# The second layer's output projection, the order of its weights and rows, and the empty rows of the expert scatter

## The chip, the core and the metric

The kernel runs on one core of a Trainium2 chip. The metric is the device time of one execution in microseconds; the time before is the median of three runs. The figures of the profile come from one more execution, recorded by the hardware profiler. TensorE (PE) multiplies, ScalarE (ACT) casts and activates, VectorE (DVE) and GpSimd (POOL) do element work, SyncE (SP) issues most of the loads; ACT and POOL issue DMAs too, POOL the indexed ones.

## The reference, cut to what matters

Two layers work on 256 latent and 256 context rows of 1024 numbers. The first layer keeps all 512 rows, the second only the 256 latent ones, which are two tiles of 128 rows (tiles 2 and 3 of the kernel). Each layer has a mixer and routed experts:

```python
gate_a, gate_b, gate_c = jnp.split(jax.nn.sigmoid(gates), N_BRANCH, axis=-1)
branch_a = (y_a @ w_glu_val) * jax.nn.sigmoid(y_a @ w_glu_gate)
m = gate_a * branch_a + gate_b * (y_b @ w_proj_gm) + gate_c * (y_c @ w_proj_da)
mix = m @ w_out                                     # w_out is 1024 x 1024
...
h_lat = layer_norm(DN_ALPHA * h_lat + g1 * mix_lat, ln1_g[l], ln1_b[l])
f_lat = modulate(layer_norm(h_lat), sh2, sc2)
# 8 of 64 experts for each row of f, each with 256 hidden units
y = sum_e weight_e * (silu(f @ w_gate[e]) * (f @ w_up[e])) @ w_down[e]   + shared expert
h_lat = layer_norm(DN_ALPHA * h_lat + g2 * y_lat, ln2_g[l], ln2_b[l])
```

## The kernel before

Dense products are made in three matmuls (`mm3`, L135 to L137): each operand is split into a rounded high part, cast by ACT, and the rest, subtracted by DVE or POOL (hi times hi, lo times hi, hi times lo). So a weight that is loaded must be cast and subtracted before PE can use it. `wload` takes a buffer of a pool with two buffers named `raw`, 8 KB per partition each, and the load into a buffer waits until the casts and subtractions of its last content are over; `wsplit` makes `whi` and `wlo`, two buffers each, out of it. Both are written by the tile framework: an engine runs its instructions in the order in which the scheduler wrote them, and waits by semaphore.

The mixer's end has three passes over eight output blocks o0 to o7 of 128 columns (`gates`): X=1, then X=0 (gate a, with w_glu_gate and w_glu_val), then X=2 (gate c, with w_proj_da, 12 matmuls of `ych`, `ycl` in each block). Each pass streams 4 MB of w_in, in four 1 MB loads of two blocks each, through the two `raw` buffers; tanh of the gate is written to `gt`. Pass X=2 leaves the sum of the three branches in `mh`, `ml`, the operand of w_out.

In the second layer w_out comes in halves of 512 columns. Half 1 is loaded by `out_weights` in four 512 KB pieces through two other buffers, `mraw`, which the modulation's weights had used; it is cast and subtracted into `wo` beside the first blocks of X=0. Half 0 is loaded after X=2's last w_in piece (two 1 MB pieces), through `raw`, and split two k-rows at a time in `whi`, `wlo`. The matmuls of both halves into the PSUM tiles `opp` run for each k as `mh` comes, a few in each block of X=2, the rest behind its last block. Then `residual` makes r = 2^0.5 h + g1 * opp in two 512-column pieces for each tile, with pieces `op_h` of the rows of h loaded for it, and `out_proj` makes both layer norms, the router's scores (sigmoid, L1041), and f, which is stored. The constants ln_g, ln_b, sh, sc are loaded from ACT's queue behind its last cast.

Routing then writes tables: `t_gather` (which row of f each of a tile's 128 places reads) and `t_scatter` (to which row of `acc` its result is added). An expert tile is two lanes of 64 places, one expert each; an expert's rows fill whole lanes, the rest of a lane stays empty. Empty places read nothing (their gather index is beyond the bounds) and scatter to 64 dump rows behind each lane's part of `acc`. For each tile, DVE copies the weights from the ring (`raw`, four slots of 3 MB, one expert each) into `gu` and `dn`, PE transposes xg (L1566), multiplies (`pg`, L1575), transposes `sg` into `ph` (L1584) and multiplies again (`py`, L1592); POOL adds the tile's 128 rows to `acc` with an indexed DMA (L1595), and SP reloads ring slots as they come free.

## Time and profile before

| | us |
|---|---|
| three runs | 2009.74, 2008.34, 2000.35 |
| median | 2008.34 |
| the profiled execution | 2000.67 |
| its span | 1998.8 |
| layer-1 mixer, 1250 to 1552 | 302 |
| its norms and router, 1552 to 1580 | 28 |
| routing, to 1618 | 38 |
| layer-1 experts, 1618 to 1957 | 339 |
| layer-0 experts, 633 to 1180 | 547 |

The profiled execution is beside the fastest of the three runs; 7.67 us lie between it and the median. Each stage is one stretch of the timeline. A wait row tells how long an engine stood still and whose event ended it. The clock column is the share of full speed that TensorE was granted: 1.00 is 2.4 GHz, 0.50 is 1.2 GHz.

### The profile page before, as it was taken

How to read it: one execution, taken by the hardware profiler on the slowest of the kernel's cores; microseconds unless marked ns; L12 is line 12 of the kernel's file. 1: busy time of each engine (PE TensorE's matmuls, PEld its weight loads, DVE VectorE, ACT ScalarE, POOL GpSimd, SP SyncE). 2: the span in 40 equal slices, each digit the busy share in tenths (PEclk: the TensorE clock that was granted, in tenths of full speed). 3: DMA queues.
4: the chain of work that ended last, by engine and by line, in shares of the span. 5: the costliest groups of instructions: out<-in, count | busy, mean ns of one | idle time of the engine just before them, and what ended most of it. 6: DMA issues, size and time to landing. Idle time of an engine off the chain costs nothing. (4 is left out here: it accounts for less than half of the span.)

```text
span 1998.8 us, 30455 instructions
## 1 busy us (share of the span) xinstructions
PE 1792.3 (90%) x10137; PEld 1040.6 (52%) x10137; DVE 1176.3 (59%) x2346; ACT 595.6 (30%) x1139; POOL 528.3 (26%) x407
## 2 busy tenths in 40 slices
PE   5798999999998999999998974989989689998894
PEld 2686876778765333333333323767789443333331
DVE  7687554333666666666665637823563666646563
ACT  3343343332222222222222215423453212221211
POOL 4354301222311222222222224321143012232221
PEclk8898999999999999999999976979999799999986
DMA  8113524453778677787898957346544379999974
GB/s 276 49 44 115 176 95 140 150 193 130 269 248 314 198 214 210 228 292 232 301 323 293 381 168 263 119 156 214 194 145 169 142 299 309 317 304 388 377 259 116
DMA packets 168310, 440.11 MB, mean 220 GB/s; under 512 B 26261, under 2 KB 82995, under 8 KB 151226
## 3 DMA queue, kind: packets, MB, share of 16 engines
q1 hardware_dynamic: 132044, 340.89, 46.6%
q0 software_dynamic: 20448, 62.41, 13.7%
q10 hardware_dynamic: 15630, 34.56, 4.8%
q8 instruction: 86, 1.41, 0.3%
q14 instruction: 102, 0.84, 0.1%
HBM read 658.36 MB, written 58.17 MB: 358 GB/s over the span
## 5 line engine op out<-in xcount | busy, mean ns | idle before, releaser
L1575 PE MATMUL pg<-gu,xt 128*64 128x512 f32 x2176 | 497.4, 610 | 1.5 <-ACT xt L1567 1.5
L1544 DVE COPY gu<-raw 128x1024 f32 x560 | 364.1, 694 | 207.8 <-SPq L1237 97.0
L1575 PEld LDWEIGHTS pg<-gu,xt 128*64 128x64 f32 x2176 | 153.8, 140 | 298.0 <-issue 283.7
L1595 POOL DMA_INDIRECT acc<-y,t_scatter x68 | 124.3, 1828 | 606.6 <-ACT ht L1585 430.0
L1592 PE MATMUL py<-dn,ht 128*64 128x512 f32 x1088 | 251.3, 604 | 5.4 <-ACT ht L1585 5.4
L1550 DVE COPY dn<-raw 128x2048 f32 x140 | 172.0, 1229 | 120.0 <-PE py L1592 100.5
L135 PE MATMUL mm<-uh,whi 128*128 128x512 f32 (+1 forms) x544 | 198.6, 365 | 6.8 <-ACT rx L848 4.6
L137 PE MATMUL mm<-uh,wlo 128*128 128x512 f32 (+1 forms) x544 | 194.9, 359 | 0.5 <-DVE wlo L314 0.5
L136 PE MATMUL mm<-ul,whi 128*128 128x512 f32 (+1 forms) x544 | 193.7, 356 | 0.0
L314 DVE TENSOR_TENSOR wlo<-raw,whi 128x1024 fp32r<-128x1024 f32 x77 | 97.8, 1271 | 114.1 <-ACT whi L311 113.9
L1579 ACT ACTIVATE sg<-pg 128x256 f32<-128x256 f32 x68 | 26.1, 384 | 452.1 <-PE pg L1575 452.1
L1524 POOL DMA_INDIRECT xg<-f,t_gather x74 | 101.0, 1365 | 180.8 <-DMA acc<-sh_y 56.2
L1592 PEld LDWEIGHTS py<-dn,ht 128*64 128x64 f32 x1088 | 72.8, 138 | 132.5 <-issue 118.7
L1594 ACT ACTIVATE y<-py,w 128x512 f32<-128x512 f32 x136 | 93.5, 687 | 161.2 <-PE py L1592 161.2
L311 ACT CAST whi<-raw 128x1024 fp32r<-128x1024 f32 x92 | 96.0, 1047 | 146.3 <-PE mm L136 117.7
L135 PEld LDWEIGHTS mm<-uh,whi 128*128 128x128 f32 x544 | 106.1, 195 | 31.7 <-issue 6.4
L137 PEld LDWEIGHTS mm<-uh,wlo 128*128 128x128 f32 x544 | 105.7, 194 | 18.5 <-issue 4.5
L136 PEld LDWEIGHTS mm<-ul,whi 128*128 128x128 f32 x544 | 106.0, 195 | 17.1 <-issue 4.5
L1566 PEld LDWEIGHTS px<-ct,xg 128*128 128x128 f32 x560 | 67.9, 194 | 57.4 <-issue 55.7
L1566 PE MATMUL px<-ct,xg 128*128 128x128 f32 x560 | 81.0, 288 | 0.9 <-DMA xg<-f,t_gather 0.9
L1567 ACT COPY xt<-px 128x512 f32<-128x512 f32 x140 | 75.3, 590 | 18.9 <-PE px L1566 17.9
L145 POOL TENSOR_TENSOR rs_r<-rs_ve,eps 128x1 f32<-128x1 f32 (+1 forms) x38 | 31.1, 822 | 178.5 <-DVE rs_ve L143 150.9
(473 smaller groups left out, 2738.8 us busy)
## 6 DMA issues: line engine op xcount, KB each, us to landing
raw<-in_w_exp_gate_dram SPq DMA_DIRECT2D x148, 1024.0 KB
raw<-in_w_exp_up_dram SPq DMA_DIRECT2D x148, 1024.0 KB
raw<-in_w_exp_down_dram SPq DMA_DIRECT2D x148, 1024.0 KB
raw<-in_w_in_dram SPq DMA_DIRECT2D x42, 1024.0 KB
mraw<-in_w_mod_dram SPq DMA_DIRECT2D x80, 512.0 KB
fraw<-in_w_mod_dram SPq DMA_DIRECT2D x16, 512.0 KB
cb_y<-acc SPq DMA_DIRECT2D x12, 512.0 KB
pj<-in_w_proj_da_dram SPq DMA_DIRECT2D x8, 512.0 KB
```

The source lines that it names most:

```text
L135: nc.tensor.matmul(out, lh, rh, start=start, stop=False)
L136: nc.tensor.matmul(out, lh, rl, start=False, stop=False)
L137: self.last = nc.tensor.matmul(out, ll, rh, start=False, stop=stop).ins
L311: self.nc.scalar.copy(hv, src)
L314: i = eng.tensor_tensor(lv, src, hv.bitcast(F32), op=ALU.subtract)
L1524: nc.gpsimd.indirect_dma_start(out=XG[t % AHEAD], out_offset=None, in_=fD, in_offset=bass.IndirectOffsetOnAxis(ap=tb["gather"][:, t:t + 1] ...
L1544: c = V.tensor_copy(GU[ln][b], gu[:, 2 * b:2 * b + 2])
L1550: c = V.tensor_copy(DN[ln][t % 2].rearrange("p a b -> p (a b)"), srcs[ln][:, 4096:6144])
L1566: nc.tensor.transpose(pX[hf][:, k * P:(k + 1) * P], XG[t % AHEAD][:, 4 * hf + k:D:8], ident)
L1575: nc.tensor.matmul(pG[t % 2][r, :], XT[t % 2][:, k, r], GU[ln][k // 2][:, k % 2].rearrange("p g n -> p (g n)"), start=(k == 0), stop=(k == ...
L1592: nc.tensor.matmul(pY[hf][r, :], HT[:, k, r], DN[ln][t % 2][:, k, 512 * hf:512 * hf + 512], start=(k == 0), stop=(k == 1), tile_position=( ...
L1595: nc.gpsimd.indirect_dma_start(out=acc, out_offset=bass.IndirectOffsetOnAxis(ap=tb["scatter"][:, t:t + 1], axis=0), in_=Y[t % 2], in_offse ...
```

## The change

In the second layer both halves of w_out are loaded and split ahead of pass X=2, in eight 512 KB pieces through the two `raw` buffers that also carry w_in. All matmuls of tile 2 are written ahead of those of tile 3. The rows of h are two tiles of 128 x 1024, and both residual pieces of a tile stand in `out_proj`. A one-column sigmoid `op_sg` behind the first tile's first norm brings ACT's table load there. In both layers the dump rows of `acc` are gone: an empty place gets an index beyond `acc` and the scatter skips it by its bounds. w_exp_down is loaded with the rows p*2 and p*2+1 in partition p, one 8 KB run; the transposes of `SG` take every second column to match.

```diff
--- before.py
+++ after.py
...
...
@@ -978,13 +977,16 @@
             nc.scalar.dma_start(dst[:, 512 * hf:512 * hf + 512], y)
             yield
 
-    def out_first(self, l, pool, tiles):
-
-        half = dict(r={}, sm={}, g={})
+    def out_first(self, l, pool, tiles, h_tiles):
+
+        half = dict(r={}, sm={}, g={}, h={})
         for s in sorted(set(t // 2 for t in tiles)):
             half["g"][s] = self.mod_bc(pool, l, 0, s, "g1_%d" % s)
         for t in tiles:
             half["r"][t] = pool.tile([P, D], F32, name="op_r%d" % t)
+            if l == DEPTH - 1:
+                half["h"][t] = pool.tile([P, D], F32, name="op_h%d" % t)
+                self.nc.sync.dma_start(half["h"][t], h_tiles[t])
             half["sm"][t] = pool.tile([P, 2], F32, name="op_sm%d" % t)
         return half
 
@@ -992,13 +994,16 @@
 
         V = self.nc.vector
         c = slice(512 * hf, 512 * hf + 512)
-        h = pool.tile([P, 512], F32, name="op_h", bufs=2 if self.l < DEPTH - 1 else 4)
-        self.nc.sync.dma_start(h, h_tile[:, c])
+        if t in half["h"]:
+            h = half["h"][t][:, c]
+        else:
+            h = pool.tile([P, 512], F32, name="op_h", bufs=2)
+            self.nc.sync.dma_start(h, h_tile[:, c])
         r = half["r"][t][:, c]
         V.tensor_mul(r, ps, half["g"][t // 2][:, c])
         V.scalar_tensor_tensor(r, h, ALPHA, r, op0=ALU.mult, op1=ALU.add, accum_out=half["sm"][t][:, hf:hf + 1])
 
-    def out_proj(self, l, pool, pp, mh, ml, wh, wl, ps1, half, tiles, t0, h_tiles, h1_tiles, f_tiles, fT, rt):
+    def out_proj(self, l, pool, pp, mh, ml, wh, wl, ps0, ps1, half, tiles, t0, h_tiles, h1_tiles, f_tiles, fT, rt):
 
         nc, A = self.nc, self.A
         V = nc.vector
@@ -1019,11 +1024,16 @@
                 ps = pp.tile([P, 512], F32, name="mm", tag="mm", bufs=2)
                 self.out_half(ps, mh, ml, wh, wl, c0)
                 self.paced(TAIL[0])
+            if l == DEPTH - 1:
+                self.residual(pool, half, t, 0, ps0[t], h_tiles[t])
             self.residual(pool, half, t, 1, ps, h_tiles[t])
             r = half["r"][t]
             sm = pool.tile([P, 1], F32, name="op_s", bufs=2)
             self.ln_two(pool, r, half["sm"][t], bc["ln1_g"], bc["ln1_b"], r, sm)
             nc.scalar.dma_start(h1_tiles[t], r)
+            if l == DEPTH - 1 and t == tiles[0]:
+
+                nc.scalar.activation(pool.tile([P, 1], F32, name="op_sg"), sm, AF.Sigmoid)
             f = pool.tile([P, D], F32, name="op_f", bufs=2)
             self.ln_two(pool, r, sm, sc2, sh2, f)
             nc.scalar.dma_start(f_tiles[t][:, 0:D], f)
@@ -1143,20 +1153,32 @@
                         ax.close()
                     mhp = pool("mhp", hx, side="right")
                     mh, ml = (mhp.tile([P, KC, n], F32R, name="mh%d" % i) for i in range(2))
+                    if not full:
+                        ow = pool("opw", hx, side="right")
+                        w0, w1 = ([ow.tile([P, KC, 512], F32R, name="wo%d%d" % (h, i)) for i in range(2)] for h in range(2))
+                        for h, w in enumerate((w0, w1)):
+                            self.out_weights(l, h, raw_tile, *w)
                     self.gates(l, gp, pp, uh, ul, t0, n, 2, yc, mT, 0, mh, ml)
                     if not full:
                         self.background(1000)
                 op = pool("opr", hx, side="right")
-                half = self.out_first(l, op, tiles)
-                ow = pool("opw", hx, side="right")
-                w1 = [ow.tile([P, KC, 512], F32R, name="wo%d" % i) for i in range(2)]
-                self.out_weights(l, 1, self.mod_raw, *w1)
+                half = self.out_first(l, op, tiles, h_tiles)
+                if full:
+                    ow = pool("opw", hx, side="right")
+                    w1 = [ow.tile([P, KC, 512], F32R, name="wo%d" % i) for i in range(2)]
+                    self.out_weights(l, 1, self.mod_raw, *w1)
                 def acc_bank(tag, bufs):
                     return pp.tile([P, 512], F32, name="opp", tag=tag, bufs=bufs)
                 free = [("att", 2), ("att", 2), ("tr", 1), ("y5", 1)]
                 ps = {t: acc_bank(*b) for t, b in zip(tiles, free)}
                 ps1 = {t: None if full else acc_bank(*b) for t, b in zip(tiles, free[2:] + free)}
-                for k in range(KC):
+
+                for t in tiles if not full else ():
+                    c = slice(t * P - t0, t * P - t0 + P)
+                    for k in range(KC):
+                        for w, p in ((w0, ps[t]), (w1, ps1[t])):
+                            self.mm3(p, mh[:, k, c], ml[:, k, c], w[0][:, k, :], w[1][:, k, :], k == 0, k == KC - 1)
+                for k in range(KC) if full else ():
                     if k % 4 == 0:
                         raw = self.wload(self.A["w_out"][l][P * k:P * k + 512, 0:512], 512)
                     if k % 2 == 0:
@@ -1164,11 +1186,7 @@
                     for t in tiles:
                         c = slice(t * P - t0, t * P - t0 + P)
                         self.mm3(ps[t], mh[:, k, c], ml[:, k, c], hv[:, k % 2, :], lv[:, k % 2, :], k == 0, k == KC - 1)
-                        if t == 2 and not full:
-                            self.mm3(ps1[t], mh[:, k, c], ml[:, k, c], w1[0][:, k, :], w1[1][:, k, :], k == 0, k == KC - 1)
-                if not full:
-                    self.out_half(ps1[3], mh, ml, *w1, 3 * P - t0)
-                for t in tiles:
+                for t in tiles if full else ():
                     self.residual(op, half, t, 0, ps[t], h_tiles[t])
             fp = pool("ftp", ox)
             fT = fp.tile([P, KC, n], F32, name="fT")
...
@@ -1214,7 +1232,7 @@
         ls = []
         for j, nm in enumerate(("w_exp_gate", "w_exp_up", "w_exp_down")):
             w = self.A[nm][l][ds(e, 1)]
-            src = w.rearrange("o (p k) n -> p (o k) n", p=P) if j < 2 else w.rearrange("o (k p) n -> p (o k) n", p=P)
+            src = w.rearrange("o (p k) n -> p (o k) n", p=P)
             o = 2048 * j
             if isinstance(slot_off, int):
                 dst = raw[:, slot_off + o:slot_off + o + 2048]
@@ -1254,11 +1272,8 @@
             nc.gpsimd.memset(x, 0.0)
         zt = pool.tile([P, D], F32, name="zt")
         nc.gpsimd.memset(zt, 0.0)
-        r0, r1 = n, LANES * (n + UNIT)
-        while r0 < r1:
-            m = min(P, r1 - r0)
-            nc.scalar.dma_start(acc[r0:r0 + m, :], zt[:m])
-            r0 += m
+        for r0 in range(n, LANES * n, P):
+            nc.scalar.dma_start(acc[r0:r0 + P, :], zt)
         M = pool.tile([P, nt, NE], F32, name="M")
 
         def tl(nm, *shape):
@@ -1474,7 +1489,7 @@
             for j in range(8):
                 nc.tensor.matmul(pl[:, 0:nx], oa[:, j, :], ob[:, j, :], start=(t == 0 and j == 0), stop=(t == nt - 1 and j == 7))
         pcc = self.C("pcol")
-        k1 = 1 if n == T else 3
+        k1 = 1 if n == T else 2
         v = pool.tile([P, nx], F32, name="lv")
         g = pool.tile([P, nx], F32, name="lg")
         V.tensor_copy(v, pl[:, 0:nx])
@@ -1482,10 +1497,8 @@
         V.scalar_tensor_tensor(g, v, -1.0, g, op0=ALU.add, op1=ALU.add)
         tb["gather"] = tab.tile([P, nx], I32, name="t_gather")
         V.tensor_copy(tb["gather"], g)
-        V.tensor_scalar(g, v, 0.5, None, op0=ALU.is_gt)
-        V.tensor_scalar(g, g, pcc[:, k1:k1 + 1], -1.0, op0=ALU.mult, op1=ALU.mult)
-        V.tensor_scalar(g, g, pcc[:, k1 + 1:k1 + 2], None, op0=ALU.add)
-        V.tensor_add(g, g, v)
+
+        V.tensor_scalar_add(g, g, pcc[:, k1:k1 + 1])
         tb["scatter"] = tab.tile([P, nx], I32, name="t_scatter")
         V.tensor_copy(tb["scatter"], g)
         return tb
@@ -1581,7 +1594,7 @@
 
             def h_t(t):
                 for k in range(2):
-                    nc.tensor.transpose(pH[:, k * P:(k + 1) * P], SG[t % 2][:, k * P:(k + 1) * P], ident)
+                    nc.tensor.transpose(pH[:, k * P:(k + 1) * P], SG[t % 2][:, k::2], ident)
                 nc.scalar.copy(HT.rearrange("p a b -> p (a b)"), pH[:, 0:256])
 
             def down(t):
@@ -1593,7 +1606,7 @@
                                              start=(k == 0), stop=(k == 1), tile_position=(0, UNIT * ln))
                     nc.scalar.activation(Y[t % 2][:, 512 * hf:512 * hf + 512], pY[hf], AF.Copy, scale=W[t % 4])
                 nc.gpsimd.indirect_dma_start(out=acc, out_offset=bass.IndirectOffsetOnAxis(ap=tb["scatter"][:, t:t + 1], axis=0),
-                                             in_=Y[t % 2], in_offset=None, compute_op=ALU.add)
+                                             in_=Y[t % 2], in_offset=None, bounds_check=LANES * n - 1, oob_is_err=False, compute_op=ALU.add)
 
             def body(t):
                 if t > 0:
...
```

SyncE, from the last pass X=0 to the routing. `raw<-in_w_in` is 1 MB of w_in, `pj` a block's other weights, `sw` the shared expert's, `wr` and `br` the router's. Before:

```order
L294 DMA pj<-in_w_glu_val_dram 128x2x256
L294 DMA raw<-in_w_in_dram 128x8x256 x3
L294 DMA pj<-in_w_proj_da_dram 128x4x256
L294 DMA raw<-in_w_in_dram 128x8x256
L294 DMA pj<-in_w_proj_da_dram 128x4x256
L294 DMA raw<-in_w_out_dram 128x4x512
L294 DMA pj<-in_w_proj_da_dram 128x4x256
L294 DMA raw<-in_w_out_dram 128x4x512
L945 DMA sw_16742<-in_w_sh_gate_dram 128x2048
```

After:

```order
L293 DMA pj<-in_w_glu_val_dram 128x2x256
L928 DMA raw<-in_w_out_dram 128x2x512 x8
L293 DMA pj<-in_w_proj_da_dram 128x4x256
L293 DMA raw<-in_w_in_dram 128x8x256 x4
L293 DMA pj<-in_w_proj_da_dram 128x4x256 x2
L944 DMA sw_16932<-in_w_sh_gate_dram 128x2048
```

The eight w_out loads stand between the last w_in piece of X=0 and the first of X=2, in the same two buffers; the two w_out loads behind X=2 and the four into `mraw` are gone.

ScalarE, at the passage from X=0 to X=2. `gt<-mm` and `gu<-mm` are the tanh of a block, `whi<-raw` the cast of a block's w_in, `wo<-raw` the casts of w_out, `mh` the cast of a finished block of X=2. Before, the row of X=0's last blocks:

```order
L311 CAST whi<-raw 128x1024
L908 ACTIVATE gt<-mm 128x256
L311 CAST whi<-pj 128x256
L912 ACTIVATE gu<-mm 128x256
L311 CAST whi<-pj 128x256
L311 CAST whi<-raw 128x1024
```

After:

```order
L933 CAST wo_16310<-raw 128x512 x2
L933 CAST wo_16312<-raw 128x512 x2
L907 ACTIVATE gt<-mm 128x256
L310 CAST whi<-pj 128x512
L911 ACTIVATE gu<-mm 128x256
L933 CAST wo_16312<-raw 128x512 x2
L310 CAST whi<-pj 128x512
L933 CAST wo_16312<-raw 128x512 x4
L310 CAST whi<-raw 128x1024 x2
```

Where a cast of X=2's first w_in blocks stood between the tanh rows of X=0, there now stand the casts of w_out, and X=2's w_in comes behind the last of them.

VectorE, at the end of the projection. `op_r_16560` and `op_r_16562` are r of tiles 2 and 3 before, `op_r_16803` and `op_r_16807` after; `g_1` is g1, `op_sm` the sum of a row. Before:

```order
L998 TENSOR_TENSOR op_r_16560<-opp,g_1_16558 128x512
L998 TENSOR_TENSOR op_r_16562<-opp,g_1_16558 128x512
L998 TENSOR_TENSOR op_r_16560<-opp,g_1_16558 128x512
L998 TENSOR_TENSOR op_r_16562<-opp,g_1_16558 128x512
L999 SCALAR_TENSOR_TENSOR op_r_16560,op_sm_16561<-op_h,op_r_16560 128x512
L999 SCALAR_TENSOR_TENSOR op_r_16562,op_sm_16563<-op_h,op_r_16562 128x512
L999 SCALAR_TENSOR_TENSOR op_r_16560,op_sm_16561<-op_h,op_r_16560 128x512
```

After:

```order
L1003 TENSOR_TENSOR op_r_16803<-opp,g_1_16801 128x512 x2
L1003 TENSOR_TENSOR op_r_16807<-opp,g_1_16801 128x512 x2
L1004 SCALAR_TENSOR_TENSOR op_r_16803,op_sm_16806<-op_h_16804,op_r_16803 128x512 x2
L1004 SCALAR_TENSOR_TENSOR op_r_16807,op_sm_16810<-op_h_16808,op_r_16807 128x512 x2
```

All four products with g1 stand first, then both additions of tile 2, then both of tile 3. On ScalarE the load of g1, which stood far ahead in the attention, now stands last in this row, behind the tanh of X=2's last block:

```order
L907 ACTIVATE gt<-mm 128x256
L1013 DMA ln_g<-in_ln_g_dram 128x1024
L1013 DMA ln_b<-in_ln_b_dram 128x1024
L279 DMA sh_1_16942<-modD_91 128x1024
L129 CAST mh_16305<-gt 128x256
L279 DMA sc_1_16944<-modD_91 128x1024
L279 DMA g_1_16801<-modD_91 128x1024
L179 ACTIVATE sp_j,sp_ss<-op_r_16803,sp_nm 128x1024
```

The constants are issued ahead of the last block's cast and not, as before, behind four more casts of w_out; g1 is the last of five.

## Rows read from the trace of the kernel before

**Rows 1.** The page: busy time of each engine, its share of the span, instructions.

```profile
PE 1792.3 (90%) x10137; PEld 1040.6 (52%) x10137; DVE 1176.3 (59%) x2346; ACT 595.6 (30%) x1139; POOL 528.3 (26%) x407
```

**Rows 2.** A stretch: us, busy PE, PEld, DVE, ACT, POOL, clock, DMA share, GB/s.

```profile
1618.00:1957.00 339.00, 310.37 (x1434) 112.73 (x1434) 204.07 (x330) 78.61 (x150) 81.12 (x48) 0.95 0.89 315
```

**Rows 3.** Waits of TensorE from 1618 to 1957: us, times, longest.

```profile
PE ph L1584 <- DVE sg L1580: 28.2, 10, 6.0
```

**Rows 4.** Waits of TensorE from 633 to 1180, layer 0's experts.

```profile
PE ph L1584 <- DVE sg L1580: 16.3, 4, 8.4
```

**Rows 5.** Waits of VectorE from 1784 to 1957; SPq signals that a load landed.

```profile
DVE gu L1544 <- SPq L1237: 44.5, 9, 10.1
```

**Rows 6.** SyncE's timeline: start, us, engine, line, operation, how many.

```profile
1459.98 2.42 SPq L929 DMA_DIRECT2D mraw<-in_w_out_dram  x2
...
1475.76 19.82 SPq L294 DMA_DIRECT2D raw<-in_w_in_dram  x3
...
1537.11 0.34 SPq L945 DMA_DIRECT2D sw<-in_w_sh_gate_dram  x1
```

**Rows 7.** ScalarE's timeline in pass X=0; brackets: idle before, and what ended it.

```profile
1463.50 1.14 ACT L934 CAST wo<-mraw 128x512 fp32r<-128x512 f32 x2 [1.12 <-DMA mraw<-in_w_out_dram]
...
1466.02 1.14 ACT L934 CAST wo<-mraw 128x512 fp32r<-128x512 f32 x2 [1.07 <-DMA mraw<-in_w_out_dram]
...
1487.73 1.05 ACT L311 CAST whi<-raw 128x1024 fp32r<-128x1024 f32 x1 [2.47 <-PE mm L136]
```

**Rows 8.** GpSimd's timeline in the same pass.

```profile
1464.20 1.46 POOL L935 TENSOR_TENSOR wo<-mraw,wo 128x512 fp32r<-128x512 f32 x1 [0.79 <-ACT wo L934]
...
1473.34 2.39 POOL L314 TENSOR_TENSOR wlo<-raw,whi 128x1024 fp32r<-128x1024 f32 x1 [0.60 <-ACT whi L311]
```

**Rows 9.** VectorE's timeline in the same pass.

```profile
1467.35 1.76 DVE L935 TENSOR_TENSOR wo<-mraw,wo 128x512 fp32r<-128x512 f32 x1
```

**Rows 10.** Stretches of 2 us behind a pause of TensorE, columns of Rows 2.

```profile
1304.00:1306.00 2.00, 2.00 (x10) 1.90 (x10) 0.29 (x1) 1.96 (x5) 0.33 (x1) 0.50 0.95 300
...
1316.00:1318.00 2.00, 2.00 (x7) 1.56 (x6) 0.42 (x1) 0.00 (x0) 1.14 (x2) 0.66 0.48 179
1318.00:1320.00 2.00, 2.00 (x39) 1.37 (x39) 0.00 (x0) 0.00 (x0) 0.33 (x1) 1.00 0.00 0
```

**Rows 11.** A stretch while the shared expert's weights load, columns of Rows 2.

```profile
1544.00:1546.00 2.00, 2.00 (x11) 1.60 (x10) 0.00 (x0) 0.97 (x1) 0.00 (x0) 1.00 1.02 420
```

**Rows 12.** ScalarE's timeline behind the projection.

```profile
1548.58 0.36 ACTq L1008 DMA_DIRECT2D ln_g<-in_ln_g_dram  x1
...
1579.29 0.22 ACT L1041 ACTIVATE sc<-rps 128x64 f32<-128x64 f32 x1 [3.27 <-PE rps L1037]
```

**Rows 13.** VectorE's timeline behind the projection.

```profile
1551.29 1.39 DVE L998 TENSOR_TENSOR op_r<-opp,g 128x512 f32<-128x512 f32 x2 [1.03 <-PE opp L137]
...
1558.53 0.69 DVE L999 SCALAR_TENSOR_TENSOR op_r<-op_h,op_r 128x512 f32<-128x512 f32 x1 [3.11 <-DMA op_h<-h]
```

**Rows 14.** Stretches of 1 us around one tile's scatter, columns of Rows 2.

```profile
1800.00:1801.00 1.00, 0.00 (x0) 0.00 (x0) 1.00 (x2) 0.00 (x0) 0.00 (x0) 0.50 0.98 414
...
1803.00:1804.00 1.00, 1.00 (x4) 0.27 (x4) 1.00 (x4) 0.27 (x1) 0.00 (x0) 0.50 1.10 287
1804.00:1805.00 1.00, 1.00 (x4) 0.24 (x2) 0.77 (x2) 0.00 (x0) 0.79 (x1) 0.50 1.05 270
...
1806.00:1807.00 1.00, 1.00 (x7) 0.28 (x4) 0.07 (x1) 0.00 (x0) 0.20 (x1) 1.00 1.04 434
```

**Rows 15.** DMA queues from 1784 to 1945: packets, MB, share; issues.

```profile
q1 hardware_dynamic: 8398, 47.17, 71.8%
q0 software_dynamic: 3168, 8.80, 23.0%
...
acc<-y,t_scatter POOLq DMA_INDIRECT x11
```

**Rows 16.** DMA queue of the indexed transfers from 1608 to 1632, and its issues.

```profile
q0 software_dynamic: 434, 1.14, 12.6%
...
xg<-f,t_gather POOLq DMA_INDIRECT x4
```

**Rows 17.** The same queue from 1955 to 1963, the last scatter alone.

```profile
q0 software_dynamic: 127, 0.51, 41.4%
```

More of the change, by code (lines that the diff above doesn't have):

```diff
@@ L69, in shape_consts @@
     for n in (T, NLAT):
-        pm, ln = p % UNIT, p // UNIT
-        cols += [1 + n + pm, ln * (n + UNIT) + n + pm]
+        cols.append(p // UNIT * n)
     for t in range(NT):
@@ L927, in out_weights @@
         for k2 in range(4):
-            raw = rp()
+            raw = rp()[:, 0:1024]
             nc.sync.dma_start(raw.rearrange("p (k n) -> p k n", k=2),
@@ L1182, in mixer @@
                 ws = self.shared_weights(l, p2)
-                self.out_proj(l, po, pp, mh, ml, w1[0], w1[1], ps1, half, tiles, t0, h_tiles, h1_tiles, f_tiles, fT, rt)
+                self.out_proj(l, po, pp, mh, ml, w1[0], w1[1], ps, ps1, half, tiles, t0, h_tiles, h1_tiles, f_tiles, fT, rt)
             hx.close()
@@ L1696, in whole @@
             fD = self.dram.tile([n, D + NE], F32, name="f_%d" % l)
-            acc = self.dram.tile([LANES * (n + UNIT), D], F32, name="acc%d" % l)
+            acc = self.dram.tile([LANES * n, D], F32, name="acc%d" % l)
             f = rows(fD, n // P)
```

## The prediction

> **What bounds the kernel now.** I read the shares first: TensorE is busy nine tenths of the span, far above the others [rows 1]. That is a mean, so next come the stages. The layer-1 mixer from 1250 to 1552 is a dense stretch of matmuls; what delays one of its passes delays the end by as much. The layer-1 experts, 1618 to 1957, move 315 GB/s with 310 of 339 us of TensorE busy [rows 2]. The waits say what ends last there: TensorE stands 28.2 us, in ten waits of up to 6.0 us, for `sg` from VectorE [rows 3], and VectorE in turn stands 44.5 us, from 1784 on, for the signal that a weight has landed [rows 5]. So from 1784 the loads bound the stage. Layer 0 has four such waits, 16.3 us [rows 4]. Between the two stands the projection's end, where a last operand decides: the last residual waits 3.11 us for a piece of h [rows 13], and the last router score comes at 1579.29 [rows 12].
>
> **Part 1, w_out ahead of X=2: a loss.** Before, the first w_in piece of X=2 is issued at 1475.76, as the first of three [rows 6], the moment when a buffer's last subtraction ends (1473.34 + 2.39 [rows 8]). Its first cast runs at 1487.73, still inside X=0 [rows 7]: pass X=2 finds its weights ready. After, eight loads of w_out take those two buffers first. What does one turn of a buffer cost? The two `mraw` loads of w_out issued at 1459.98 and 2.05 us later (2.42 less one issue of about 0.37; together one row) [rows 6] are cast at 1463.50 and 1466.02 [rows 7], 3.5 and 4.0 us after issue. The casts take 1.14 us, and the subtraction behind the first of them ends at 1464.20 + 1.46 = 1465.66 on GpSimd [rows 7, 8], 2.2 us after the cast began; one on VectorE took 1.76 us [rows 9], so up to 2.8. A turn is 5.7 to 6.8 us; I take 6.4, or 3.2 us for each load over two buffers. The first load gets its buffer at 1475.8, the second when X=0's last block is subtracted, about 1485 (the cast of that block runs one behind the 1487.73 one, 5.2 us earlier, and its subtraction ends some 2.3 us later). Three more turns from there, for loads four, six and eight, bring the eighth to 1485 + 19 = 1504, and X=2's first piece follows in the other buffer at about 1504.5. A 1 MB piece lands about 5.6 us later (4.0 plus another 512 KB at the 400 GB/s of this stretch, with margin), the cast takes 1.05 [rows 7] and the subtraction about 1.2: X=2 starts near 1512 instead of 1496. Following the whole pass in the new order by such durations, I find 18 us of added TensorE idle time, 13 of it in one piece ahead of X=2. The number of matmuls is unchanged, and each waits no less. The bounds: 10 us, if the loads land faster than the `mraw` ones and casts are never late; 21, at 6.8 us a turn.
>
> Behind a pause TensorE's clock falls: after the pause that ends before 1304 the rows show 0.50 while it is busy all the time, and 1.00 again only from 1318 [rows 10]. A stretch at 0.50 costs half its length: the pauses in the expert stage, of 6 us, leave a stretch at 0.50 from 1800 to past 1805 [rows 14], with some 3 us of it busy. That brackets the cost at 1.5 to 6.5 us; I take 3. **Part 1: +21 us, from +10 to +27.**
>
> **Part 2, the norms' operands: a loss.** Before, the shared weights are issued at 1537.11 [rows 6], when the last gate block has been read, and move at 420 GB/s [rows 11]; they are over long before the constants start at 1548.58 [rows 12], and these end with the pieces of h, the last of which is used at 1558.53 [rows 13]. That is 7.2 us behind the last `opp` (1551.3), and the router's last score 20.8 us behind that. After, 3.6 MB of shared and router weights, 2.6 MB of constants with g1 among them, and 1 MB of h all start together at the end of the last gate block, which is now 7 to 8 us ahead of the last `opp` and no longer 14, since half of the projection no longer runs behind it. 7.15 MB at about 405 GB/s are 17.6 us, plus 2 for issue and the first bytes: 12 us behind the last `opp` they are in. VectorE then has four products and four additions, of 0.69 us each [rows 13], with g1 as the last constant ahead of all of them: about 4 us, part of it under the rest of the loads. Only then starts the chain of about 21 us. So the score comes at 12 + 4 + 21 = 37 us behind the last `opp`, and not at 28: **+9 us, from -3** (loads of ACT's queue get ahead of the shared weights, and the early large pieces of h help) **to +12.** The table load that moves is 1.28 us in the timeline and hides either before or after; I give it nothing.
>
> The Trainium skill, "DMA: Bandwidth & Descriptors", section "Specifications", gives 358 GB/s as the limit of one core's share of HBM; the 420 GB/s of the row is above it, so the trace disagrees. By the page's figure the 7.15 MB would take 20 us and this part would be +11.5.
>
> **Part 3, empty rows not scattered: a gain.** What does a scatter cost where loads bound? At 1800 the loads alone move 414 GB/s, during the scatter all queues together 270 to 287, and behind it 434 [rows 14]. Four microseconds at 65 to 70% of the rate is some 1.5 us of lost load bytes by that count, and more, about 2.5 us, when the scatter's own bytes are taken off. The one scatter that runs alone, 127 packets, takes 41.4% of 8 us = 3.3 us of the engines [rows 17]. Does skipping a row save its packet? The gather skips already: four gathers of layer 1 moved 1.14 MB [rows 16], where 512 rows of 4352 bytes would be 2.23 MB. So yes, as far as reads tell. How many rows are empty: 25 tiles of 128 places hold 2048 rows in layer 1, 36% empty; 43 tiles hold 4096 rows in layer 0, 26% empty. Layer 1 saves 0.36 x 2.5 = 0.9 us of DMA time for each tile; twelve tiles run in the bound stretch, 1784 to 1945, where loads took 71.8% of the engines and indexed transfers 23.0% [rows 15]. 12 x 0.9 = 11 us, plus 2 for the slow clock that follows each wait. Layer 0: 0.26 x 2.5 = 0.65 us each, but its loads bind only in its last quarter: 10 tiles, 6 us. From both sides: nothing, if the loads wait for slots rather than for bytes, up to all of the 28.2 and 16.3 us [rows 3, 4] with their slow clock, 55. **-19 us, from 0 to -45.** Fewer zeroing stores, three fewer table operations and a shorter last scatter: -1.
>
> On arbitration the Trainium skill, same page, section "Queues, rings and completion order", says that each engine takes turns between queues at packet granularity. By that rule a packet that is skipped gives its turn to a load, which agrees with the rate falling to 287 during a scatter; the sum stays.
>
> w_exp_down in 8 KB runs instead of 4 KB: the gate and up weights have such runs already and landed no faster in the 420 GB/s stretch [rows 11] than the down weights. Nothing, the same for the transposes with a stride.
>
> **The sum.** +21 + 9 - 19 - 1 = +10, against the profiled 2000.67: 2010.7. The median of the runs lies 7.7 us above that execution, so the same sum on it gives 2018.3; with the halves of a microsecond that I cut in parts 1 and 2, **2019 us**.
>
> **The rivals.** (a) *The scatter was all of the expert waits.* The loads then catch up and 44.5 us of TensorE's waits go, with some of the clock: -45 + 30 - 1, 1992 us: faster. For it: VectorE's waits for loads are larger than TensorE's. Against: the loads also carry 47 MB, three quarters of the engines' time, which nothing removes. It decides once a skipped row frees more than 1.5 times what I take. Chance 0.2. (b) *Nothing in the experts.* If a skipped row is still written as a descriptor, or the ring's slots decide, the loss stands alone: +29, 2037. Chance 0.15. (c) *The edit does what it says*, the ring does not hold X=2 up: then w_out is ready early, part 1 is nothing, and the sum is -11: 1997. The order speaks against it, ScalarE can't cast X=2's weights ahead of w_out's, and SyncE can't load them; it needs a landing below 1.5 us, which no load here shows. Chance 0.05. (d) *The losses are at their lower bounds*, +10 and 0, against 19: within 10 us, 2000 to 2015. Chance 0.25. My forecast, +5 to +18, has 0.35.
>
> **Chances and range.** A difference of 0.5%, 10 us, is about what a measurement of this kernel can tell from no change. Faster: (a) and (c), less their weak ends, 0.22. Within: (d) and the lower part of the forecast, 0.33. Slower: the rest with (b), 0.45. The range leaves out the far halves of (a) and (b): 1990 to 2036.
>
> **What would show it.** Right: a pause of TensorE of 10 us or more between X=0 and X=2 of layer 1, with 0.50 in the clock behind it; the casts `wo` 3 us apart for each pair; X=2's first w_in load issued at or after 1500 on the scale of before; products with g1 that wait for a DMA and a last score about 37 us behind the last `opp`; the packets of the indexed queue down by a fifth or more, and waits for `sg` in layer 1 down from 28 us to some 15. Wrong: X=2 that starts without a pause, expert waits that vanish, or an indexed queue with as many packets as before.

## The result and the profile after

The changed kernel takes 2010.64 us (median of 20 runs) where the kernel before takes 2003.27 (20 runs): slower by 7.4 us by the medians. The recorded ratio is 1.006, interval 1.0039 to 1.0082, which would be 8 to 16 us; a loss under one per cent, clear of no change, whose size is known only roughly. The forecast was slower by 10.7. The forecast's absolute number, 2019, lies 8.4 us higher than the measured one; 5.1 of these are that the first three runs of before had a median above that of twenty. Runs of the kernel before lie up to 0.8% from their median, so a single profile's difference is good to a few microseconds, and the stages below are read by their own rows.

The profiled execution's span is 2007.9 us, 9.1 more than before. Cut at marks that both traces have, the difference goes like this:

| stretch | before | after | difference |
|---|---|---|---|
| start to the first tile of layer 0 | 631.4 | 634.4 | +3.0 |
| layer 0's experts, first `px` to last `ph` | 539.9 | 533.9 | -6.0 |
| on to the moment X=0 hands its first buffer over | 304.5 | 301.3 | -3.2 |
| from there to the start of the last `opp` | 75.8 | 97.0 | +21.2 |
| to the last router score | 27.7 | 40.0 | +12.3 |
| routing | 37.5 | 36.6 | -0.9 |
| layer 1's experts | 339.9 | 323.1 | -16.8 |
| the end | 42.1 | 41.6 | -0.5 |

The mark between the third and the fourth row moves itself: X=0 hands its buffer over 2.3 us sooner after the attention's last matmul (`att`) than before, since half of w_out is no longer cast beside its first blocks. From that last `att` to the start of the last `opp` the way is 118.4 us before and 137.3 after, 18.9 more. The five traces with w_out loaded as before give 118.4 to 118.9, the five with the change's eight loads through `raw` 135.3 to 137.5.

SyncE's timeline around the passage from X=0 to X=2 (start, us, engine, line, operation, how many), to be laid beside [rows 6]:

```profile
1469.57 25.27 SPq L928 DMA_DIRECT2D raw<-in_w_out_dram  x8
...
1497.90 22.42 SPq L293 DMA_DIRECT2D raw<-in_w_in_dram  x4
...
1560.09 0.34 SPq L944 DMA_DIRECT2D sw<-in_w_sh_gate_dram  x1
...
1572.11 0.80 SPq L989 DMA_DIRECT2D op_h<-h  x2
```

The buffer that X=2's first piece got before now goes to w_out; X=2 gets its first piece 28.3 us later. ScalarE's casts in that stretch, beside [rows 7]:

```profile
1488.55 1.14 ACT L933 CAST wo<-raw 128x512 fp32r<-128x512 f32 x2 [1.86 <-DMA raw<-in_w_out_dram]
...
1491.68 1.14 ACT L933 CAST wo<-raw 128x512 fp32r<-128x512 f32 x2 [0.93 <-DMA raw<-in_w_out_dram]
...
1498.02 1.14 ACT L933 CAST wo<-raw 128x512 fp32r<-128x512 f32 x2 [2.22 <-DMA raw<-in_w_out_dram]
1506.27 1.99 ACT L310 CAST whi<-raw 128x1024 fp32r<-128x1024 f32 x2 [7.11 <-DMA raw<-in_w_in_dram]
```

TensorE's waits from 1460 to 1625 (what waited, for what, us, times, longest), and its clock in stretches of 2 us (the column ahead of the DMA share; the first pair after the length is busy PE):

```profile
PE tf L1043 <- DVE rs_ve L142: 27.3, 1, 27.3
PE mm L134 <- ACT whi L310: 15.7, 1, 15.7
```

```profile
1488.00:1490.00 2.00, 0.00 (x0) 0.00 (x0) 0.39 (x2) 1.45 (x4) 1.44 (x2) 0.98 0.31 72
1490.00:1492.00 2.00, 1.65 (x6) 1.36 (x6) 1.88 (x3) 1.07 (x3) 0.51 (x1) 0.50 0.51 199
...
1508.00:1510.00 2.00, 2.00 (x11) 2.00 (x11) 1.71 (x2) 0.26 (x1) 0.00 (x0) 0.50 0.03 9
1510.00:1512.00 2.00, 2.00 (x17) 2.00 (x16) 0.69 (x1) 0.62 (x1) 0.00 (x0) 0.90 0.53 106
1512.00:1514.00 2.00, 1.25 (x11) 1.05 (x9) 0.00 (x0) 0.83 (x1) 0.00 (x0) 1.00 1.07 382
```

One pause of 15.7 us stands ahead of X=2 (the 27.3 us are TensorE's wait for the norms). The clock falls to 1.2 GHz at 1490, behind two microseconds without a matmul, and is back at 2.4 GHz only from about 1510.4, with some 5 us of matmuls between. VectorE behind the projection, beside [rows 13]:

```profile
1579.43 2.48 DVE L1003 TENSOR_TENSOR op_r<-opp,g 128x512 f32<-128x512 f32 x4 [15.69 <-DMA g<-modD]
1581.83 0.68 DVE L1004 SCALAR_TENSOR_TENSOR op_r<-op_h,op_r 128x512 f32<-128x512 f32 x1
```

All four products stand still for g1. It was issued late, and h later still. At the end of the gates SyncE issues the shared weights from 1560.09 on and ScalarE the first constant at 1560.10, but g1 follows only at 1567.84 and h at 1572.11. SyncE waited for two of its own loads to land ahead of h; what held g1's issue the trace does not tell (ScalarE's issue of g1, then the waits of SyncE's queue):

```profile
1567.84 0.33 ACTq L279 DMA_DIRECT2D g<-modD  x1
```

```profile
SPq L1196 <- DMA sw<-in_w_sh_gate_dram: 5.3, 1, 5.3
SPq L989 <- DMA sw<-in_w_sh_up_dram: 4.4, 1, 4.4
```

In the experts the waits of [rows 3, 4, 5] have become these (TensorE in layer 1, in layer 0; VectorE from 1784 to 1967):

```profile
PE ph L1597 <- DVE sg L1593: 16.3, 4, 5.7
```

```profile
PE ph L1597 <- DVE sg L1593: 8.4, 2, 4.9
```

```profile
DVE gu L1557 <- SPq L1255: 30.4, 8, 8.1
```

And the indexed queue, over the whole kernel in the page of before and of after (packets, MB, share of the engines):

```profile
q0 software_dynamic: 20448, 62.41, 13.7%
```

```profile
q0 software_dynamic: 20448, 51.95, 11.1%
```

The scatter of [rows 17] is not the last but the last but one, and the row's window ends before its last packets. The same scatter whole, before (1957 to 1965) and after (1966 to 1974.5):

```profile
DMA packets 152, 0.61 MB, mean 76 GB/s; under 512 B 16, under 2 KB 16, under 8 KB 144
...
q0 software_dynamic: 144, 0.52, 42.5%
```

```profile
DMA packets 154, 0.46 MB, mean 54 GB/s; under 512 B 58, under 2 KB 58, under 8 KB 144
...
q0 software_dynamic: 144, 0.35, 29.9%
```

A skipped row saves its 4 KB, not its packet: the counts of the queue are equal to the last one, and in the scatter 58 of the packets have under 512 bytes, where 16 had before. The engines' time for it falls from 42.5% of 8 us = 3.4 us to 29.9% of 8.5 us = 2.5. The gather had done the same all along. One in the kernel before (1906 to 1912), which moves 0.16 MB, some 37 rows of its 128 places, has 144 packets too:

```profile
q0 software_dynamic: 144, 0.16, 7.5%
```

### The profile page after: what moved, and what is told of

Read it like the earlier page. It is cut to its first block, busy times and chain, and to the rows that moved or that the text cites. A ratio compares the mean times of both kernels' runs of the same rounds, so it can differ in the third digit from the quotient of the medians.

```text
span 2007.9 us, 30524 instructions
## 1 busy us (share of the span) xinstructions
PE 1786.8 (89%) x10137; PEld 1049.0 (52%) x10137; DVE 1177.0 (59%) x2341; ACT 596.5 (30%) x1144; POOL 524.3 (26%) x410
## 3 DMA queue, kind: packets, MB, share of 16 engines
q0 software_dynamic: 20448, 51.95, 11.1%
## 5 line engine op out<-in xcount | busy, mean ns | idle before, releaser
L1588 PE MATMUL pg<-gu,xt 128*64 128x512 f32 x2176 | 491.4, 605 | 1.9 <-ACT xt L1580 1.9
L1563 DVE COPY dn<-raw 128x2048 f32 x140 | 171.8, 1227 | 137.3 <-PE py L1605 116.5
L134 PE MATMUL mm<-uh,whi 128*128 128x512 f32 (+1 forms) x544 | 199.0, 366 | 23.3 <-ACT whi L310 15.8
L310 ACT CAST whi<-raw 128x1024 fp32r<-128x1024 f32 x88 | 91.8, 1048 | 153.8 <-PE mm L135 128.0
L1537 POOL DMA_INDIRECT xg<-f,t_gather x74 | 93.8, 1268 | 162.7 <-DVE t_scatter L1503 56.2
L134 PEld LDWEIGHTS mm<-uh,whi 128*128 128x128 f32 x544 | 106.3, 195 | 48.8 <-ACT whi L310 18.9
L144 POOL TENSOR_TENSOR rs_r<-rs_ve,eps 128x1 f32<-128x1 f32 (+1 forms) x38 | 31.3, 825 | 191.1 <-DVE rs_ve L142 164.1
```

Of the source, the lines that this page charges most:

```text
L134: nc.tensor.matmul(out, lh, rh, start=start, stop=False)
L1537: nc.gpsimd.indirect_dma_start(out=XG[t % AHEAD], out_offset=None, in_=fD, in_offset=bass.IndirectOffsetOnAxis(ap=tb["gather"][:, t:t + 1] ...
L1563: c = V.tensor_copy(DN[ln][t % 2].rearrange("p a b -> p (a b)"), srcs[ln][:, 4096:6144])
L1588: nc.tensor.matmul(pG[t % 2][r, :], XT[t % 2][:, k, r], GU[ln][k // 2][:, k % 2].rearrange("p g n -> p (g n)"), start=(k == 0), stop=(k == ...
```

## The experiments

Ratios are to the kernel before on the same chip. "Tail" is the way from the last `opp` to the last router score in the trace, 27.7 us before and 40.0 after.

**Skipped rows alone, in the kernel before.**

```diff
-                                             in_=Y[t % 2], in_offset=None, compute_op=ALU.add)
+                                             in_=Y[t % 2], in_offset=None, bounds_check=LANES * n - 1, oob_is_err=False, compute_op=ALU.add)
```

(with the table, the smaller `acc` and its zeroing as in the change)

> The kernel before with the empty scatter rows skipped and nothing else. Theory: the profiled gain behind the router (18.2 us in layer 1, 6.2 in layer 0, between the profiles of before and after) is the skipped rows', so this kernel is 18 to 28 us faster than before, near 1979 us where before is 2003, and its waits of TensorE for sg fall from 28.2 and 16.3 us to below 18 and 10. Rival: the gain is that of the 8 KB runs of w_exp_down; then this kernel gains under 8 us and keeps the waits.

Measured: 1979.17 us, ratio 0.9896 (0.9866 to 0.9926), 21 us faster. TensorE's waits, layer 1 and layer 0:

```profile
PE ph L1578 <- DVE sg L1574: 13.1, 4, 4.8
```

```profile
PE ph L1578 <- DVE sg L1574: 9.1, 3, 5.1
```

Layer 1's experts take 323.8 us, 16.1 less than before: nearly all of the change's 16.8 there. The theory holds. In layer 0 the experts take 531.4, 8.5 less; how much of this is the skipped rows' is open, since traces with one and the same expert code (the changed kernel and the five runs below that leave its experts alone) spread there from 531.9 to 539.3.

**The changed kernel without it** (the same lines taken back).

> The changed kernel without the skipped rows: empty places scatter to dump rows as before. Theory: the whole loss stands, 33 us up to the router's last score, and the experts gain nothing: 25 to 37 us slower than before, some 2033 where before is 2003. Rival: the 8 KB runs of w_exp_down made the experts' gain; then it is slower than before by 7 to 15 us, like the changed kernel.

Measured: 2031.23 us, ratio 1.0148 (1.0113 to 1.0182). In its trace the mixer is 19.5 us longer than before and the tail 11.8, 31.3 together. The experts, with the 8 KB runs of w_exp_down now alone, are 4.0 us shorter than before in layer 1 (335.9) and 4.4 in layer 0; the waits are 23.3 and 9.8 us. That the runs help is not shown by this: the six traces with the changed kernel's own expert code spread from 322.4 to 328.9 us in layer 1. The skipped rows' 16 us there are clear of that spread.

**w_out in buffers of its own, in the changed kernel.**

```diff
-                            self.out_weights(l, h, raw_tile, *w)
+                            self.out_weights(l, h, self.mod_raw, *w)
```

> The changed kernel with the eight w_out loads in the two buffers mraw, where half of them went before, in place of the two that carry w_in. Theory: the pause of 15.7 us ahead of pass X=2 and the slow clock behind it are the shared buffers', so the pause falls below 3 us and the time by 15 to 22 us against the changed kernel, to 1989 to 1996 where before is 2003. Rival: the pause is ScalarE's and the subtractions' sheer work, or the load rate; then the same eight pieces delay X=2 here too and the pause stays above 10 us.

Measured: 1993.48 us, ratio 0.9969 (0.9937 to 1.0001), some 15 us (medians) to 18 us (ratios) better than the changed kernel. TensorE's waits from 1450 to 1560 are now all of this:

```profile
PE mm L134 <- ACT gt L907: 7.6, 8, 2.2
PE mm L136 <- DVE wlo L313: 0.4, 1, 0.4
```

The pause is gone; the eight pieces are cast beside X=0's tanh rows. The pause was the two shared buffers', not ScalarE's work, which is the same here. From the last `att` to the last `opp` it takes 121.9 us, where the changed kernel takes 137.3 and the kernel before 118.4: 15.4 of the 18.9 us were the buffers'. The other 3.5 go with waits for `gt`, the tanh that stands in one row with the casts: 8.9 us in this stretch, and 10.6 in the kernel below with all three mended (122.1), where before has 7.3. Here the rest is slower matmuls, with the clock at 0.88 from 1459 to 1469.

**g1 early, in the changed kernel.**

```diff
+                        g1 = {1: self.mod_bc(pool("g1p", hx, side="right"), l, 0, 1, "g1_1")}
                         ow = pool("opw", hx, side="right")
```

> The changed kernel with g1 loaded ahead of w_out into a place of its own, as before, and nothing else moved. Theory: the 12 us longer way from the last opp to the router's last score is the loads' queue, in which g1 is only the last; the products of 2.5 us go under the wait, 0.5 MB less is loaded, and the score comes 3 to 5 us earlier. Rival: g1 alone holds the residual; then the score comes 9 to 12 us earlier and the wait for a DMA ahead of the residual is gone.

Measured: 2008.96 us, ratio 1.0042 (1.0013 to 1.007). Tail 38.0: 2.0 us sooner, less than expected, and not the rival's 9. The wait has only changed its name:

```profile
1568.41 2.48 DVE L1003 TENSOR_TENSOR op_r<-opp,g 128x512 f32<-128x512 f32 x4 [2.58 <-PE opp L136]
1581.84 0.69 DVE L1004 SCALAR_TENSOR_TENSOR op_r<-op_h,op_r 128x512 f32<-128x512 f32 x1 [10.95 <-DMA op_h<-h]
```

**h ahead of the shared expert's weights, in the changed kernel** (a queue order without a wait, `self.order(x, self.hrow)` for the three loads).

> The changed kernel with the rows of h issued ahead of the shared expert's weights on SyncE's queue. Theory: the longer way from the last opp to the router's last score (39.7 us, 27.4 before) is the 7.2 MB that all start at the end of the gates, of which 3 MB aren't needed until the shared expert; behind them the products wait 15.7 us for g1. With them last, g1 and h land some 6 us sooner and the score comes 32 to 35 us behind the last opp: 5 to 8 us faster than the changed kernel. Rival: the two queues share the engines evenly whatever stands first on SyncE's, so g1, last on ScalarE's, lands no sooner: under 2 us.

Measured: 2014.69 us, ratio 1.0083 (1.0055 to 1.0111), no gain; tail 37.7, 2.3 us sooner. It is still g1 that is late:

```profile
1582.82 2.48 DVE L1006 TENSOR_TENSOR op_r<-opp,g 128x512 f32<-128x512 f32 x4 [13.04 <-DMA g<-modD]
```

The rival, under 2 us, was nearly right: against the last `opp` g1 is issued 4.9 us sooner than in the changed kernel, but it landed 13.9 us after its issue, where there it took 11.6, in spite of the order on SyncE's queue.

**One of the three shared weights loaded.** `[self.one_load(v, A[nm][l])] * 3` in place of three loads; the other two are left out, so the second layer's shared expert is not the reference's.

> The changed kernel with one of the shared expert's three weight loads in the second layer; the other two, 2 MB, are left out and the one tile is used in their place, so the second layer's shared expert isn't the reference's. Putting h ahead of them gained only 2 us, with g1 landing as late as before. Theory: what holds g1 is the sum of the bytes that start at the end of the gates, whatever their order; 2 MB less at 405 GB/s lets g1 land 5 us sooner, and the score comes 34 to 36 us behind the last opp instead of 40. Rival: g1 waits for its own queue's four loads and its place on ScalarE; then the score stays within 1.5 us of 40.

Measured: 2016.23 us, ratio 1.0069 (1.0038 to 1.0101); tail 37.4. This lies between the two: 2 MB less gave 2.6 us and not 5. The trace shows one more reason for h: SyncE issued it only when an earlier load had landed, as in the changed kernel (waits of SyncE's queue).

```profile
SPq L995 <- DMA sw<-in_w_sh_gate_dram: 5.8, 1, 5.8
```

So bytes count, and the sum of bytes is not the whole: from 1572 to 1582 the core moved 256 to 367 GB/s, less than the 405 of the sum. Why the loads were slower there stays open.

**All three mended at once**: w_out's own buffers, g1 early, h ahead.

> The changed kernel with w_out in buffers of its own, g1 loaded early, and the rows of h ahead of the shared weights. Theory: the pause ahead of X=2 stays away (-18 against the changed kernel), g1 early and h ahead give some 4 us of the norms' 12: 1985 to 1991 where before is 2000, still behind the kernel with skipped rows alone (1979 there), since the loads still start 7 us before the last opp and no matmul is saved. Rival: tile-by-tile order with both halves split early shortens the way to the router once its loads are not late; then 1970 to 1976, ahead of it.

Measured: 1987.7 us, ratio 0.9947 (0.9925 to 0.997). The time is as the theory said; the split is not: tail 31.5, 8.5 us sooner than in the changed kernel, where the two edits alone gave 2.0 and 2.3 and w_out's own buffers 0.1. (The profiled execution, 2001.69 us, is the slowest of its ten; the tail is read by its own rows.) The residual needs g1 and h both, so one of them early only hands the wait to the other. Two parts of the change, the matmuls' order by tiles and the moved table load, were taken back by no run. Here h lands last, with a wait of 4.4 us:

```profile
1565.25 0.69 DVE L1007 SCALAR_TENSOR_TENSOR op_r<-op_h,op_r 128x512 f32<-128x512 f32 x1 [4.43 <-DMA op_h<-h]
```

**Rows of h ahead in the kernel before, with skipped rows.**

```diff
+            if l == DEPTH - 1:
+                half["h"][t] = pool.tile([P, D], F32, name="op_h%d" % t)
+                self.nc.sync.dma_start(half["h"][t], h_tiles[t])
```

> The kernel before with the empty rows skipped and the rows of h as two whole tiles loaded ahead (what the change says of them), w_out and the matmuls' order as before. Theory: the last residual no longer waits 3.1 us for a piece of h, 0.5 MB less is loaded behind the projection: the score comes 24 to 26 us behind the last opp in place of 27.2, and the kernel is 1 to 4 us faster than the one with skipped rows alone, near 1976 where before is 2001. Rival: the norms' constants hold that place anyway; then nothing moves, 27 us and 1979.

Measured: 1979.11 us, ratio 0.9911 (0.9889 to 0.9933). Tail 23.6, 4.0 us sooner than with skipped rows alone, since the rows are now issued in the attention, at 1306 and 1314, and the additions follow the products without a wait:

```profile
1543.32 0.68 DVE L1004 SCALAR_TENSOR_TENSOR op_r<-op_h,op_r 128x512 f32<-128x512 f32 x1
```

In the whole time 4 us don't stand out: the intervals of 0.9896 and 0.9911 overlap.

**Skipped rows and 8 KB runs, and sg sorted.** First the change's own two lines on w_exp_down in the kernel before:

> The kernel before with the empty rows skipped and w_exp_down in 8 KB runs, with sg transposed by every second column. Theory: that transpose's weight load takes 206 ns and not 141, so a tile that waits for nothing takes 12.13 us and not 12.06, 4 us in 68 tiles; the longer runs give back about as much in waits: within 3 us of the kernel with skipped rows alone. Rival: the longer runs gain in load time what they gained without the skipping (waits of 28.2 and 16.3 us down to 23.3 and 9.8): 5 us faster or more.

Measured: 1979.06 us, ratio 0.992 (0.9894 to 0.9946), level with skipped rows alone. Then with h ahead and sg written sorted:

```diff
-                nc.scalar.activation(SG[t % 2], pG[t % 2][:, 0:EH], AF.Silu)
-                V.tensor_mul(SG[t % 2], SG[t % 2], pG[t % 2][:, EH:2 * EH])
+                nc.scalar.activation(SG[t % 2].rearrange("p (k j) -> p j k", k=2), pG[t % 2][:, 0:EH].rearrange("p (j k) -> p j k", k=2), AF.Silu)
+                V.tensor_mul(SG[t % 2], SG[t % 2], pG[t % 2][:, EH:2 * EH].rearrange("p (j k) -> p k j", k=2))
```

> The rows of h ahead, empty rows skipped, w_exp_down in 8 KB runs, and sg written sorted (even columns, then odd ones) by ScalarE and VectorE, so that its transposes read 128 neighbouring columns again. Theory: the weight loads fall back to 141 ns and the tile to 12.06 us; the longer runs are then a pure gain: 2 to 6 us faster than the kernel with skipped rows and whole rows of h, 1971 to 1975 where before is 2001. Rival: writing sg with a stride costs ScalarE and VectorE on the way to the transposes what it saves TensorE: no faster.

Measured: 1973.87 us, ratio 0.9891 (0.9864 to 0.9918). The transposes' weight loads in layer 1 (least, median, most ns; first and last start), without and with the sorting:

```profile
L1578 PEld LDWEIGHTS ph<-ct,sg x50: 194/206/219, 1628.8 to 1938.6; 128*128 128x128 f32 x50
```

```profile
L1584 PEld LDWEIGHTS ph<-ct,sg x48: 138/142/225, 1630.1 to 1925.1; 128*128 128x128 f32 x48
```

Two starts of `ph` that waited for nothing, 12.13 us apart without the sorting, then 12.06 with it:

```profile
1703.90 0.50 PE L1578 MATMUL ph<-ct,sg 128*128 128x128 f32 x2
...
1716.03 0.50 PE L1578 MATMUL ph<-ct,sg 128*128 128x128 f32 x2
```

```profile
1702.44 0.44 PE L1584 MATMUL ph<-ct,sg 128*128 128x128 f32 x2
...
1714.50 0.44 PE L1584 MATMUL ph<-ct,sg 128*128 128x128 f32 x2
```

The stride's price in a tile is shown: 55 of the 67 steps from one tile's `ph` to the next are 12.13 us without the sorting, 55 are 12.06 with it. Its sum, some 5 us in 68 tiles, and what the runs give are within the spread (0.9891 against 0.9911 without runs and sorting). ScalarE's silu takes 672 ns with the sorted writing and not 383, without making the tile longer. This kernel is faster than both the kernel before, by 22 us, and the changed one.

## Why the prediction was right, point by point

**Part 1, w_out ahead of X=2: right in place, a little high.** Forecast +21 us; from the last `att` to the last `opp` it measures +18.9. Behind the hand-over of X=0's buffer the stretch grew by 21.2, but X=0 had become 2.3 us faster ahead of it, which the forecast left out. X=2's first piece was issued at 1497.90, which is 1504.1 on the scale of before (the traces run 6.2 us apart there), forecast 1504.5; the casts come 3 us apart. The piece is cast 8.4 us after its issue where 5.6 were taken, and X=2 starts at 1513.6 on that scale and not at 1512. The buffers of its own, which took the pause and 15.4 us with it, show that the shared buffers were the cause. The clock: about 5 us of matmuls at half speed cost some 2.5 us, taken as 3.

**Part 2, the norms' operands: right in sign, low by 3.** Forecast +9 with a bound of +12; measured +12.3. In the forecast's own terms, 12 + 4 + 21 us behind the last `opp` have become 12.8 + 4.2 + 23.0: g1 lands at 1579.43 (`opp` 1566.6), the last addition starts at 1583.66, the last score at 1606.63. So the term that was too small is the chain. Its 21 were read behind the last addition of before (1558.53), but there ScalarE had begun tile 2's first norm 3 us ahead of that, at 1555.51; in the changed order both tiles' additions come first. And the table load, taken at nothing, stands on the way: ScalarE loads the table when the mean of tile 2's second norm is ready (1589.20), and the pass over the row starts behind it:

```profile
1589.40 1.28 ACT L1036 ACT_TABLE_LOAD   x1 [3.51 <-DVE sp_nm L172]
...
1590.81 1.13 ACT L179 ACTIVATE sp_j<-op_r,sp_nm 128x1024 f32<-128x1024 f32 x1
```

What moving the load costs in the whole was not measured apart. The landing has the forecast's size and not its course: the loads don't all start together, but the core moves 393 to 424 GB/s from 1566 to 1578 all the same. The lower bound, that early pieces of h help, had no ground: the change's text asks for early rows, and the trace has them behind the shared weights.

**Part 3, the skipped rows: right in size, wrong on the packets.** Forecast -19 and -1; measured -21 alone. In the changed kernel layer 1's experts take 16.8 us less and layer 0's 6.0, with waits of 16.3 us in layer 1 where some 15 were forecast. (The upper bound stands as 55 in the working and as 45 in the range; neither was near.) The forecast had the indexed queue's packets down by a fifth and named an unchanged count as a sign of being wrong; they are the same 20448. The step that failed is the reading of [rows 16]: bytes that go down don't tell that packets do. Its 434 packets of 4352 bytes would be 1.89 MB, and the row has 1.14; they are those of three gathers, 144 each (the fourth is issued only at 1627.67). So the gather was the right likeness, and the trace of before already held the short packets. The working that the prediction based on the Trainium skill's "DMA: Bandwidth & Descriptors", section "Queues, rings and completion order" (a packet that is skipped gives its turn to a load), doesn't describe what happens here: the turn is taken by a short packet, and what the loads win is its bytes. Rival (b)'s condition, a skipped row that is still written, came true without its consequence.

**w_exp_down in 8 KB runs and transposes with a stride, taken at nothing: wrong on the stride, open on the runs.** The stride costs 65 ns for each weight load and 0.07 us in a tile, some 5 us in 68. What the runs give is not clear of the spread: with the stride's cost in them the two expert stages are 4.0 and 4.4 us shorter than before where nothing else relieves the loads, and with skipped rows 3.5 and 2.0 us longer than without runs and stride. Rows of before could have told of the stride: the transposes of `xg` read with a stride of eight, and the page gives their weight loads 194 ns, where those of `ph`, of the same 128 x 128, took 141 ns in the trace of before.

**The sum.** That the difference came out within 3.3 us of the forecast's is in part luck: part 1 was 2 us too high, part 2 3 too low, and the experts gained 22.8 in the trace where 19 were forecast. By the forecast's own scale a difference under 10 us is hardly to be told from none.

**The rivals.** The larger expert gain didn't come: with skipped rows 13.1 and 9.1 us of waits remain. That the expert stage gains nothing (b), and that the w_out loads hide (c), are out by the runs above. Rival (d)'s time, 2000 to 2015, holds the result, but not by its small losses: they are 18.9 and 12.3 us, and the gain is larger than its 19.

## What to carry to other kernels

A load that is moved ahead takes its buffers from whoever stood there: count the turns of the ring that it passes, not the loads' bytes. Where an operation needs two late operands, make both early or leave both; one alone moves the name in the wait row and little else. When a change bundles a gain with a loss of the same size, as here 21 against 31, time each part by itself before keeping or dropping the whole. Where a row of the profile gives packets and bytes, divide one by the other before reading one as the other.

## What the runs showed of the hardware

A row that an indexed scatter skips by its bounds still goes out as a packet of under 512 bytes: 144 packets for 128 places with the skipping and without, 58 and 16 of them short. An indexed gather does the same, 144 packets for 0.16 MB. The saving of the scatter is in bytes (62.41 to 51.95 MB) and engine time (13.7% to 11.1%). A weight load of TensorE that reads every second column of an fp32 tile takes 206 ns where neighbouring columns take 141 or 142. ScalarE's silu that writes the columns sorted takes 672 ns in place of 383, VectorE's product behind it 411 ns in both.
